# Scores of two heads on different rows of the TensorE array, with keys kept without zero rows

## The chip, the cores and the metric

The kernel runs on one core of a Trainium2 chip. The metric is the time of one execution on the device in microseconds. The core has the engines TensorE (PE, with PEld for its weight loads), VectorE (DVE), ScalarE (ACT), GpSimd (POOL) and the queue SP, which issues transfers.

## What is computed

Two layers of a block on x of 256 x 1024 in f32 come first: a gated feed-forward network, a mixer of three attentions, and a second feed-forward network. Behind them stand a third block (a state-space mixer and short convolutions) and a mixture of experts, which the change leaves alone. The mixer, cut to what matters:

```python
h = rmsnorm(x, mix_norm[l]) @ w_in[l]
o_a = mla_mixer(h_a, ...)    # 6 heads, keys of 64 + 32 columns
o_b = nsa_mixer(h_b, ...)    # 6 heads of 64 columns in 2 key groups of 3 heads
o_c = diff_mixer(h_c, ...)   # 4 heads, each with 2 score products of 32 columns
x = x + jnp.concatenate([o_a, o_b, o_c], axis=-1) @ w_out[l]

# nsa: head (g, r) uses the keys of group g
s_cmp = einsum(q, k_cmp) * scale                 # 15 compressed keys a group
p_cmp = softmax(where(cmp_mask, s_cmp, NEG_BIG)) * cmp_mask
# selection: with 4 blocks of 64 tokens all blocks are taken, so it is causal attention with ks, vs
# window: 512 is longer than the 256 tokens, so it is causal attention with kw, vw
o = g0 * o_cmp + g1 * o_slc + g2 * o_win         # gates from h

# diff
o = softmax(q1 k1) v - lam * softmax(q2 k2) v, then rmsnorm over the head's 64 columns
```

## The kernel before

Everything runs on one core; tokens are two tiles of 128. `_mixer` (line 519) runs once per layer. Its steps stand in a string, `ORDER` (line 40): `w...` are groups of columns of w_in, `mp`, `np` and `dp` prepare the mla, nsa and diff heads, `m0` to `m5`, `n0` to `n5` and `d0` to `d3` are one head each, `df` closes the diff heads. The program's text gives each instruction a place, and a planner in the compiler puts the instructions of each engine into one order by that place and by when their inputs come; so an instruction of a later step can fill a hole of an earlier one. Tiles with a tag share so many buffers, and an instruction that needs a new buffer waits until the old one has been read.

PSUM has eight banks: in the mixer S has 3, T (transposes) 2, O (outputs of a pair of heads) 1, W 2 (line 313). Scores of one head stand in one S bank: queries of token tile 1 against all keys (columns 0 to 255 or 271), queries of tile 0 against the first keys, and masks that are added by a product of an identity with a bf16 mask (`scores`, line 744; `nsa_head`, line 842, for the scores with the 16 compressed columns in front). VectorE then takes maxima (line 725), ScalarE the exponentials with sums (line 729), VectorE and GpSimd scale the rows (line 739), TensorE transposes the probabilities (`ptp`, line 691), VectorE or ScalarE copies them to PT, and the products with the values of two heads write different halves of one O bank (`pv_pair`, line 705; `in_turns`, line 712, keeps such products together behind the first).

An nsa query tile holds two heads, one on rows 0 to 63 and one on rows 64 to 127; a diff query tile holds four score heads of 32 rows. So that a product over all 128 rows gives one head's scores, the keys stand in tiles with zeros on the other rows: `ks` and `kw` (lines 802 to 805), one version per group, filled by half (lines 819, 820), and `kC` (lines 892 to 905), four versions of each of two tiles, filled by quarters by VectorE and ScalarE from the transposed keys `kct` in an S bank. GpSimd writes the zeros.

After the heads, `wo` (lines 972 to 981) multiplies by w_out in four column blocks of two halves; a half stands in a W bank, the other in an S bank. Its eight row chunks are taken in the order `KO`; chunks 3 to 5 are the nsa heads, written in pairs by `store_o`. `fetch` and `cols` issue the transfers on SP into four buffers `st`; `split` makes a high and a low part of each weight on ScalarE and VectorE.

Of the kernel before, what the change touches and what calls it, by code (L numbers as in the profile page):

```python
# [18 lines left out]
T = 256  # L19
# [3 lines left out]
KD = 8  # L23
# [15 lines left out]
LOW.update({k: "vp" for k in ["h3", "g2"]})  # L39
ORDER = "w01 w5 w2 mp m0 m1 w8 w3 w4 w6 np w7 dp m2 m3 d0 d1 n0 n1 d2 d3 n2 n3 n4 n5 m4 df m5"  # L40


class Block:
# [475 lines left out]
    def _mixer(self, l, xops, after):  # L519
# [224 lines left out]
        def scores(s, q, k, kw):  # L744
# [4 lines left out]
            self.mm(s[:, C0], self.identb, self.maskb, False, True)  # L749

        blocks = lambda P: [P[:, i * 128:(i + 1) * 128] for i in range(3)]
        halves = lambda v: [v[:, t * 128:(t + 1) * 128] for t in range(2)]
# [17 lines left out]
        def nsa_prepare():  # L770
# [30 lines left out]

            ks = ap.tile([128, 2, 16 + T], F32, name="ks", tag="hA")
            kw = ap.tile([128, 2, T], F32, name="kw", tag="cqT")
            nc.gpsimd.memset(ks, 0.0)
            nc.gpsimd.memset(kw, 0.0)

# [9 lines left out]
            ACT(qT[:, 2], p2[:, 0:256], scale=0.125)  # L816
            for g in range(2):
                q = slice(g * 64, (g + 1) * 64)
                nc.vector.tensor_copy(ks[q, g, 16:16 + T], p3[q, 0:256])
                nc.vector.tensor_copy(kw[q, g], p3[q, 256:512])  # L820
            p, p2 = self.bank("T", "kcmp"), self.bank("S", "vcmp")
            vcmp = ap.tile([16, 128], F32, name="vcmp", tag="vcmp")
            for g in range(2):
                self.mm(p[g * 64:(g + 1) * 64, 0:15], w2[0:64], h1[0:64, 1, g * 15:(g + 1) * 15])
                self.mm(p2[0:15, g * 64:(g + 1) * 64], h1[64:128, 1, g * 15:(g + 1) * 15], w2[64:128], g == 0, True)
            for g in range(2):
                ACT(ks[g * 64:(g + 1) * 64, g, 0:15], p[g * 64:(g + 1) * 64, 0:15], scale=0.5)
            ACT(vcmp[0:15], p2[0:15, 0:128], scale=0.5)
# [12 lines left out]
                (slice(0, 128), slice(288, 416)), (slice(128, 384), slice(16, 272))]  # L841
        def nsa_head(h):
            qT, ks, kw, vcmp, gt = nsa
            g, hg = divmod(h, 3)
            qt = halves(qT[:, hg])
            im, mb = self.identb, self.maskb

            s = self.bank("S", "S")
            self.mm(s[:, 0:272], qt[1], ks[:, g], True, False)
            self.mm(s[:, 0:16], im, self.cmask[:, 1], False, False)  # L850
            self.mm(s[:, 144:272], im, mb, False, False)
            self.mm(s[:, 272:416], qt[0], ks[:, g, 0:144], False, False)
            self.mm(s[:, 272:288], im, self.cmask[:, 0], False, False)
            self.mm(s[:, 288:416], im, mb, False, True)
            P = ap.tile([128, 416], F32, name="P", tag="P", bufs=6)
            scale_rows(P, SEGC, softmax(s, P, SEGC, gt[:, h, 0:4], -1e29), "c")
            p, pt, n = transposes(blocks(P), "ptp")
            nc.scalar.copy(pt, p[:, 0:n])
            p2 = self.bank("T", "ptc")
            cpt = ap.tile([16, T], F32, name="cpt", tag="cpt", bufs=2)  # L860
            for t in range(2):
                tr(p2[0:16, t * 128:(t + 1) * 128], P[:, 384 + t * 16:400 + t * 16], ident)
            nc.vector.tensor_copy(cpt, p2[0:16, 0:T])
            vc = slice(128 + g * 64, 192 + g * 64)
            pv("s", pt, [hV[:, t, vc] for t in range(2)])
            waiting.setdefault("c", []).append((cpt, vcmp[0:15, g * 64:(g + 1) * 64]))
            if h % 2:
                o = self.bank("O", "opair")
                pv_pair(o, "s", True, False)
                c0, c1 = waiting.pop("c")  # L870
                in_turns([lambda o_=o_, c=c: self.mm(o_, c[1], c[0][0:15], False, False)
                          for o_, c in ((o[64:128, 0:256], c1), (o[0:64, 0:256], c0))])
            s = self.bank("S", "S")
            scores(s, qt, kw[:, g], kw[:, g, 0:128])
            P = ap.tile([128, 384], F32, name="P", tag="P", bufs=6)
            scale_rows(P, SEGS, softmax(s, P, SEGS, gt[:, h, 4:6]), "w")
            p, pt, n = transposes(blocks(P), "ptp")
            nc.vector.tensor_copy(pt, p[:, 0:n])
            vc = slice(256 + g * 64, 320 + g * 64)
            pv("w", pt, [hV[:, t, vc] for t in range(2)])  # L880
            if h % 2:
                pv_pair(o, "w", False, True)
                store_o(3 + h // 2, o[:, 0:256])


        def diff_prepare():
            for t in range(2):
                self.rope(hC[:, t].rearrange("p (h c) -> p h c", h=16)[:, :, 0:8]
                          .rearrange("p h (i f) -> p h i f", i=2), 16, 4, t)
            qC = ap.tile([128, 2, T], F32, name="qC", tag="qC")  # L890

            kC = [ap.tile([128, 4, T], F32, name="kC", tag=tag) for tag in ("kC0", "hC")]
            for k in kC:
                nc.gpsimd.memset(k, 0.0)
            p, p2 = self.bank("T", "qct"), self.bank("S", "kct")
# [12 lines left out]
            return qC, kC, po, pov  # L908

        def diff_head(h):  # L910
            qC, kC, po, pov = dif
            c = h // 2
            Ps = []
            for j in range(2):
                k = kC[c][:, 2 * (h % 2) + j]
                s = self.bank("S", "S")
# [36 lines left out]
        for step in steps:  # L953
# [10 lines left out]
            elif step[0] == "w":  # L964
                w_in_groups([int(c) for c in step[1:]])
                for _ in step[1:]:
                    fetch()
            else:
                {"m": mla_head, "n": nsa_head, "d": diff_head}[step[0]](int(step[1]))
# [947 lines left out]
```

## Time and profile before

| | |
|---|---|
| median of 3 runs | 1529.91 us (1529.60 to 1532.09) |
| the profiled execution | 1532.0 us |
| its span | 1529.8 us |
| TensorE busy | 1492.0 us, 98% of the span |
| VectorE busy | 1025.1 us, 67% |
| ScalarE busy | 729.7 us, 48% |
| GpSimd busy | 91.4 us, 6% |

The profile is of one execution. Busy time is the time in which an engine has an instruction in work, and a busy TensorE is not one at its peak. The chain of waits goes back from the last instruction to what released each step. A view by stretch gives busy time per engine between two moments; an engine that is full in a stretch sets its length, and a share over the whole span can hide that.

### The profile page before, as it was taken

The page shows a single profiled execution, that of the slowest core. Times are in us where ns is not written, and L with a number is a line of the kernel's source. Part 1 is how long each engine was busy: PE and PEld are TensorE (multiplying, and loading weights), DVE is VectorE, ACT ScalarE, POOL GpSimd, SP SyncE. Part 2 cuts the span into 40 slices and gives each one's busy share as a digit, 9 for nine tenths or more (in the row PEclk, how much of TensorE's full clock was granted, in tenths as well). Part 3 has the DMA queues.
Part 4 walks back from the last instruction along what each step waited for, and adds up shares of the span by engine and source line. Part 5 has one row for each costly group of instructions (what it writes and reads, how often), then busy time and mean ns, then how long its engine had stood idle before and what let it go on. Part 6 is the DMA issues. An engine that isn't in the chain of part 4 may idle for free.

```text
span 1529.8 us, 25415 instructions
## 1 busy us (share of the span) xinstructions
PE 1492.0 (98%) x9970; PEld 1253.6 (82%) x9970; DVE 1025.1 (67%) x2013; ACT 729.7 (48%) x1382; POOL 91.4 (6%) x142
## 2 busy tenths in 40 slices
PE   8999999999999999999999999999899999999996
PEld 7999998788999989999888999999799987344432
DVE  6886775868677786778576877779988875122112
ACT  6555565755454555455665655547554442011011
POOL 0000000520000000000025000000510100000000
PEclk9999999999999999999999999999999999999999
DMA  7756664216555565655640555566533588999993
GB/s 252 246 175 193 189 164 145 78 56 205 186 188 193 167 193 192 193 192 164 169 130 2 193 185 176 192 192 207 153 123 116 189 296 336 359 393 393 393 394 117
DMA packets 223559, 308.93 MB, mean 202 GB/s; under 512 B 20908, under 2 KB 167608, under 8 KB 223432
## 3 DMA queue, kind: packets, MB, share of 16 engines
q1 hardware_dynamic: 223128, 306.71, 60.1%
q8 instruction: 80, 1.31, 0.4%
q10 hardware_dynamic: 304, 0.53, 0.1%
q14 instruction: 47, 0.39, 0.1%
HBM read 306.16 MB, written 1.05 MB: 201 GB/s over the span
## 4 chain that ended last, share of the span: by engine, by line
PE 92%; DVE 5%; ACT 1%; issue 1%; DMA 0%; POOL 0%; ACTq 0%; DVEq 0%
PE gu L98 32%; PE acc L98 16%; PE proj L98 6%; PE win L98 6%; PE gate L98 4%; PE y L98 4%; PE up L98 4%; PE h L98 3%; PE wo L98 3%; PE S L98 3%; PE moe L98 1%; PE opair L98 1%; PE ptp L691 1%; PE zp L98 1%; PE xgp L98 1%; DVE wl L167 1%
## 5 line engine op out<-in xcount | busy, mean ns | idle before, releaser
L167 DVE TENSOR_TENSOR wl<-st,wh 128x1024 fp32r<-128x1024 f32 (+1 forms) x370 | 447.5, 1220 | 198.9 <-ACT wh L166 187.7
L166 ACT ACTIVATE wh<-st 128x1024 fp32r<-128x1024 f32 (+1 forms) x382 | 399.3, 1059 | 336.5 <-PE gu L98 134.4
L98 PE MATMUL gu<-xhl,wh 128*128 128x512 f32 (+1 forms) x1440 | 487.8, 392 | 3.1 <-ACT wh L166 2.2
L98 PE MATMUL gu<-xhl,wl 128*128 128x256 f32 x1408 | 381.6, 280 | 0.0
L98 PEld LDWEIGHTS gu<-xhl,wh 128*128 128x128 f32 x1440 | 268.2, 190 | 61.0 <-ACT wh L166 2.6
L98 PEld LDWEIGHTS gu<-xhl,wl 128*128 128x128 f32 x1408 | 260.8, 189 | 0.3
L98 PE MATMUL acc<-hx,wh 128*128 128x256 f32 x1408 | 252.1, 281 | 0.0
L98 PEld LDWEIGHTS acc<-hx,wh 128*128 128x128 f32 x1408 | 216.3, 188 | 1.6
L98 PE MATMUL acc<-hx,wl 128*128 128x256 f32 x704 | 196.8, 281 | 0.0
L98 PE MATMUL proj<-uhl,wh 128*128 128x272 f32 (+2 forms) x592 | 127.6, 306 | 5.3 <-DVE dv L1184 1.6
L98 PEld LDWEIGHTS acc<-hx,wl 128*128 128x128 f32 x704 | 132.6, 188 | 0.0
L98 PE MATMUL win<-wh,xhl 128*128 128x256 f32 (+1 forms) x576 | 109.7, 286 | 0.2 <-DVE xT L410 0.2
L98 PEld LDWEIGHTS proj<-uhl,wh 128*128 128x128 f32 x592 | 95.9, 191 | 10.5 <-ACT cv L1222 2.8
L98 PE MATMUL proj<-uhl,wl 128*128 128x272 f32 (+2 forms) x328 | 95.0, 290 | 0.0
L98 PEld LDWEIGHTS win<-wh,xhl 128*128 128x128 f32 x576 | 90.8, 191 | 4.2 <-issue 3.4
L98 PE MATMUL win<-wl,xhl 128*128 128x256 f32 (+1 forms) x288 | 81.9, 284 | 0.0
L394 ACT ACTIVATE hx<-up 128x512 fp32r<-128x512 f32 x44 | 27.7, 630 | 87.8 <-DVE up L393 87.8
L98 PEld LDWEIGHTS proj<-uhl,wl 128*128 128x128 f32 x328 | 62.5, 191 | 0.2
L1814 DVE SCALAR_TENSOR_TENSOR ys<-y,rc,ys 128x512 fp32r<-128x512 f32 x16 | 11.7, 749 | 67.2 <-ACT ys L1634 66.8
L739 POOL TENSOR_SCALAR P<-P,mx 128x128 f32<-128x128 f32 (+2 forms) x88 | 53.2, 621 | 57.9 <-DVE mx L732 41.8
L729 ACT ACTIVATE P<-S,mx 128x256 f32<-128x256 f32 (+2 forms) x128 | 48.9, 394 | 13.4 <-DVE mx L725 3.6
L98 PEld LDWEIGHTS win<-wl,xhl 128*128 128x128 f32 x288 | 55.0, 191 | 0.3
(522 smaller groups left out, 2133.7 us busy)
## 6 DMA issues: line engine op xcount, KB each, us to landing
st<-ffn_wg SPq DMA_DIRECT2D x44, 1024.0 KB, 5.7
st<-ffn_wu SPq DMA_DIRECT2D x44, 1024.0 KB, 5.4
st<-ffn_wd SPq DMA_DIRECT2D x44, 1024.0 KB, 4.7
st<-w_in SPq DMA_DIRECT2D x36, 1024.0 KB, 5.4
st<-w_out SPq DMA_DIRECT2D x16, 1024.0 KB
mf<-expert_w_gate SPq DMA_DIRECT2D x25, 512.0 KB, 9.8
mf<-expert_w_down SPq DMA_DIRECT2D x21, 512.0 KB, 10.7
mf<-expert_w_up SPq DMA_DIRECT2D x18, 512.0 KB, 11.3
```

What stands on the lines that cost most here:

```text
L98: return self.nc.tensor.matmul(out, lhsT, rhs, start=start, stop=stop, skip_group_check=True)
L166: hi = self.nc.scalar.activation(hl[0], src, AF.Copy)
L167: sub = (self.nc.gpsimd if lo[i] == "p" else self.nc.vector).tensor_sub(hl[1], src, hl[0].bitcast(F32))
L394: nc.scalar.activation(hh, up, AF.Copy)
L691: tr(p[:, i * 128:(i + 1) * 128], b, ident)
L729: nc.scalar.activation(P[:, d], s[:, c], AF.Exp, bias=m[:, 0, i:i + 1], accum_out=m[:, 1, i:i + 1])
L739: (nc.gpsimd if key + str(i) in "c0 c1 c2 d0 d1 m0 w0 w1".split() else nc.vector).tensor_scalar(P[:, d], P[:, d], r[:, i:i + 1], None, op0 ...
L1814: V.scalar_tensor_tensor(yl, py[half], rc[:, 1:2], yh.bitcast(F32), op0=OP.mult, op1=OP.subtract)
```

## The change

Scores of two heads that stand on different rows of the query tile are now issued in turns, each into an S bank of its own: for nsa the heads (0, r) and (1, r) on rows 0 to 63 and 64 to 127, for diff the two score heads of a head, 32 rows each. The product goes over a head's own rows, so the keys need no zeros: `ks`, `kw` and `kC` are single tiles, their memsets go (but for one column of `ks`), and their copies from PSUM are one instruction each. An nsa step is now a pair of heads from both groups; so output chunk 3 + r holds heads r and 3 + r, and w_out's rows are loaded in that order, in four transfers per block in place of one. `ORDER` has three nsa steps in place of six. The diff, cut to its core:

```diff
-ORDER = "w01 w5 w2 mp m0 m1 w8 w3 w4 w6 np w7 dp m2 m3 d0 d1 n0 n1 d2 d3 n2 n3 n4 n5 m4 df m5"
+ORDER = "w01 w5 w2 mp m0 m1 w8 w3 w4 w6 np w7 dp m2 m3 d0 d1 n0 d2 d3 n1 n2 m4 df m5"
...
+        def scores_pair(banks, q, k, rows):
+
+            in_turns([lambda s=s, r=r, c=c, t=t, n=n: self.mm(s[:, c], q[t][r], k[r, 0:n], t == 1, False)
+                      for t, c, n in ((1, C1, 256), (0, C0, 128)) for s, r in zip(banks, rows)])
+            for s in banks:
+                self.mm(s[:, 128:256], self.identb, self.maskb, False, False)
+                self.mm(s[:, C0], self.identb, self.maskb, False, True)
...
-            ks = ap.tile([128, 2, 16 + T], F32, name="ks", tag="hA")
-            kw = ap.tile([128, 2, T], F32, name="kw", tag="cqT")
-            nc.gpsimd.memset(ks, 0.0)
-            nc.gpsimd.memset(kw, 0.0)
+            ks = ap.tile([128, 16 + T], F32, name="ks", tag="hA")
+            kw = ap.tile([128, T], F32, name="kw", tag="cqT")
+            nc.gpsimd.memset(ks[:, 15:16], 0.0)
...
-            for g in range(2):
-                q = slice(g * 64, (g + 1) * 64)
-                nc.vector.tensor_copy(ks[q, g, 16:16 + T], p3[q, 0:256])
-                nc.vector.tensor_copy(kw[q, g], p3[q, 256:512])
+            nc.vector.tensor_copy(ks[:, 16:16 + T], p3[:, 0:256])
+            nc.vector.tensor_copy(kw, p3[:, 256:512])
...
-            for g in range(2):
-                ACT(ks[g * 64:(g + 1) * 64, g, 0:15], p[g * 64:(g + 1) * 64, 0:15], scale=0.5)
+            ACT(ks[:, 0:15], p[:, 0:15], scale=0.5)
...
-        def nsa_head(h):
+        def nsa_pair(hg):
...
+            rows = [slice(64, 128), slice(0, 64)]
+
+            two = [self.bank("S", "S") for _ in range(2)]
+            in_turns([lambda s=s, r=r, t=t, c=c, n=n: self.mm(s[:, c:c + n], qt[t][r], ks[r, 0:n], t == 1, False)
+                      for t, c, n in ((1, 0, 272), (0, 272, 144)) for s, r in zip(two[::-1], rows)])
+            for s in two:
+                self.mm(s[:, 0:16], im, self.cmask[:, 1], False, False)
+                self.mm(s[:, 144:272], im, mb, False, False)
+                self.mm(s[:, 272:288], im, self.cmask[:, 0], False, False)
+                self.mm(s[:, 288:416], im, mb, False, True)
+            for g, s in enumerate(two):
+                h = 3 * g + hg
...
+            two = [self.bank("S", "S") for _ in range(2)]
+            scores_pair(two[::-1], qt, kw, rows)
+            for g, s in enumerate(two):
...
+            pv_pair(o, "w", False, True)
+            store_o(3 + hg, o[:, 0:256])
...
-            kC = [ap.tile([128, 4, T], F32, name="kC", tag=tag) for tag in ("kC0", "hC")]
-            for k in kC:
-                nc.gpsimd.memset(k, 0.0)
+            kC = ap.tile([128, 2, T], F32, name="kC", tag="kC0")
...
-            for c in range(2):
-                for i in range(4):
-                    q = slice(i * 32, (i + 1) * 32)
-                    (nc.vector.tensor_copy if i % 2 else nc.scalar.copy)(kC[c][q, i], p2[q, c * T:(c + 1) * T])
+            nc.vector.tensor_copy(kC, p2[:].rearrange("p (c t) -> p c t", c=2))
...
-            for j in range(2):
-                k = kC[c][:, 2 * (h % 2) + j]
-                s = self.bank("S", "S")
-                scores(s, halves(qC[:, c]), k, k[:, 0:128])
+            two = [self.bank("S", "S") for _ in range(2)]
+            r0 = h % 2 * 64
+            scores_pair(two[::-1], halves(qC[:, c]), kC[:, c], [slice(r0 + 32, r0 + 64), slice(r0, r0 + 32)])
+            for s in two:
...
-        wo = [self.cols(a["w_out"][l], (b * 256, b * 256 + 256)) for b in range(4)]
+
+        def wo_unit(b):
+
+            st = self.wp.tile([128, 2048], F32, name="st", tag="st", bufs=4)
+            v = st[:].rearrange("p (k n) -> p k n", n=256)
+            w = a["w_out"][l][:, b * 256:(b + 1) * 256]
+            rows = lambda r, n, p: w[r:r + n, :].rearrange("(k p) c -> p k c", p=p)
+            nc.sync.dma_start(v[:, 0:3], rows(0, 384, 128))
+            for g in range(2):
+                nc.sync.dma_start(v[g * 64:(g + 1) * 64, 3:6], rows(384 + g * 192, 192, 64))
+            self.loaded = nc.sync.dma_start(v[:, 6:8], rows(768, 256, 128)).ins
+            return st, KD, 256
+
+        wo = [wo_unit(b) for b in range(4)]
```

## Rows read from the trace of the kernel before

**Rows 1.** The page, busy time of engines: us, share of the span, instructions.
```profile
PE 1492.0 (98%) x9970; PEld 1253.6 (82%) x9970; DVE 1025.1 (67%) x2013; ACT 729.7 (48%) x1382; POOL 91.4 (6%) x142
```

**Rows 2.** Windows, layer 0: length, busy PE PEld DVE ACT POOL (count), clock, DMA.
```profile
283.00:300.00 17.00, 17.00 (x138) 13.77 (x137) 15.77 (x73) 13.68 (x64) 10.85 (x17) 1.00 0.01 2
300.00:316.30 16.30, 16.30 (x134) 13.07 (x133) 15.05 (x68) 11.21 (x51) 13.13 (x23) 1.00 0.01 2
316.30:328.60 12.30, 12.30 (x105) 10.33 (x103) 3.91 (x8) 2.41 (x5) 0.00 (x0) 1.00 0.00 1
328.60:342.20 13.60, 13.60 (x115) 13.60 (x114) 10.07 (x18) 9.55 (x14) 0.00 (x0) 1.00 0.34 102
```

**Rows 3.** The same view for layer 1, its second softmax stretch.
```profile
812.70:829.00 16.30, 16.30 (x134) 13.07 (x133) 14.15 (x68) 11.23 (x51) 12.23 (x22) 1.00 0.01 2
```

**Rows 4.** Timeline of TensorE, preparation: start, us, operation, [idle before <-releaser].
```profile
274.90 0.39 PE L98 MATMUL vcmp<-w,h 64*15 64x64 f32 x4 [0.95 <-DVE h L798]
275.23 0.66 PE L900 MATMUL kct<-ident,hC 128*128 128x128 f32 x4
...
278.44 0.70 PE L98 MATMUL S<-kC,qC 128*128 128x256 f32 x2 [0.85 <-ACT P L729]
```

**Rows 5.** Chain that ended last, layer 0: start us, us, what.
```profile
286.25 0.92 PE S L98 x8
...
288.94 1.70 PE S L98 x12
...
297.99 0.80 PE opair L98 x8
298.80 0.48 PE ptp L691 x3
...
306.66 0.34 PE ptp L691 x3
```

**Rows 6.** Timeline of TensorE: the end of one window score set.
```profile
300.60 0.22 PE L98 MATMUL S<-maskb,identb 128*128 128x128 bf16 x1
300.65 0.44 PE L98 MATMUL S<-kw,qT 128*128 128x128 f32 x2
300.93 0.22 PE L98 MATMUL S<-maskb,identb 128*128 128x128 bf16 x1
300.99 0.68 PE L98 MATMUL S<-ks,qT 128*128 128x272 f32 x2
```

**Rows 7.** Instructions on the score tile S: count, ns min/median/max, first and last start.
```profile
L725 DVE TENSOR_REDUCE mx<-S x128: 152/292/422, 250.0 to 824.0; 128x1 f32<-128x128 f32 x52, 128x1 f32<-128x256 f32 x52, 128x1 f32<-128x16 f32 x24
...
L98 PE MATMUL S<-kC,qC x64: 275/354/483, 278.4 to 806.8; 128*128 128x256 f32 x32, 128*128 128x128 f32 x32
```

**Rows 8.** Timeline of VectorE, preparation, columns as in rows 4.
```profile
273.10 0.42 DVE L819 COPY ks<-ktb 64x256 f32<-64x256 f32 x1
...
274.66 0.19 DVE L798 SCALAR_TENSOR_TENSOR h<-h,h 64x30 f32<-64x30 f32 x1
276.31 0.42 DVE L905 COPY kC<-kct 32x256 f32<-32x256 f32 x1 [1.47 <-ACT kC L905]
...
280.67 0.43 DVE L905 COPY kC<-kct 32x256 f32<-32x256 f32 x1
...
281.68 0.55 DVE L762 COPY PT<-ptp 128x384 f32<-128x384 f32 x1
```

**Rows 9.** VectorE's waits, 283 to 316.3 us: total us, times, longest.
```profile
DVE mx L725 <- PE S L98: 1.4, 4, 0.5
```

**Rows 10.** Timeline of the SP queue: DMA issues, start and us.
```profile
238.32 20.70 SPq L150 DMA_DIRECT2D st<-w_out  x4
265.31 0.37 SPq L150 DMA_DIRECT2D st<-ffn_wg  x1
```

**Rows 11.** Instructions on the tile wo: count, ns, first and last start.
```profile
L98 PE MATMUL wo<-ohl,wh x256: 278/283/386, 287.7 to 854.5; 128*128 128x256 f32 x128
```

More of the change, by code (lines that the diff above doesn't have):

```diff
@@ L841, in _mixer @@
                 (slice(0, 128), slice(288, 416)), (slice(128, 384), slice(16, 272))]
-        def nsa_head(h):
+        def nsa_pair(hg):
             qT, ks, kw, vcmp, gt = nsa
-            g, hg = divmod(h, 3)
             qt = halves(qT[:, hg])
             im, mb = self.identb, self.maskb
-            s = self.bank("S", "S")
[L849 to L883, printed above, removed]
@@ new lines, in nsa_pair @@
+            for g, s in enumerate(two):
+                h = 3 * g + hg
+                P = ap.tile([128, 416], F32, name="P", tag="P", bufs=6)
+                scale_rows(P, SEGC, softmax(s, P, SEGC, gt[:, h, 0:4], -1e29), "c")
+                p, pt, n = transposes(blocks(P), "ptp")
+                nc.scalar.copy(pt, p[:, 0:n])
+                p2 = self.bank("T", "ptc")
+                cpt = ap.tile([16, T], F32, name="cpt", tag="cpt", bufs=2)
+                for t in range(2):
+                    tr(p2[0:16, t * 128:(t + 1) * 128], P[:, 384 + t * 16:400 + t * 16], ident)
+                nc.vector.tensor_copy(cpt, p2[0:16, 0:T])
+                pv("s", pt, [hV[:, t, 128 + g * 64:192 + g * 64] for t in range(2)])
+                waiting.setdefault("c", []).append((cpt, vcmp[0:15, g * 64:(g + 1) * 64]))
@@ new lines, in nsa_pair @@
+            o = self.bank("O", "opair")
+            pv_pair(o, "s", True, False)
+            c0, c1 = waiting.pop("c")
+            in_turns([lambda o_=o_, c=c: self.mm(o_, c[1], c[0][0:15], False, False)
+                      for o_, c in ((o[64:128, 0:256], c1), (o[0:64, 0:256], c0))])
+            two = [self.bank("S", "S") for _ in range(2)]
+            scores_pair(two[::-1], qt, kw, rows)
+            for g, s in enumerate(two):
+                P = ap.tile([128, 384], F32, name="P", tag="P", bufs=6)
+                scale_rows(P, SEGS, softmax(s, P, SEGS, gt[:, 3 * g + hg, 4:6]), "w")
+                p, pt, n = transposes(blocks(P), "ptp")
+                nc.vector.tensor_copy(pt, p[:, 0:n])
+                pv("w", pt, [hV[:, t, 256 + g * 64:320 + g * 64] for t in range(2)])
@@ L913, in diff_head @@
             Ps = []
-            for j in range(2):
-                k = kC[c][:, 2 * (h % 2) + j]
-                s = self.bank("S", "S")
-                scores(s, halves(qC[:, c]), k, k[:, 0:128])
+            two = [self.bank("S", "S") for _ in range(2)]
+            r0 = h % 2 * 64
+            scores_pair(two[::-1], halves(qC[:, c]), kC[:, c], [slice(r0 + 32, r0 + 64), slice(r0, r0 + 32)])
+            for s in two:
                 P = ap.tile([128, 384], F32, name="P", tag="P", bufs=6)
@@ L968, in _mixer @@
             else:
-                {"m": mla_head, "n": nsa_head, "d": diff_head}[step[0]](int(step[1]))
+                {"m": mla_head, "n": nsa_pair, "d": diff_head}[step[0]](int(step[1]))
         KO = [int(c) for c in "01345672"]
-        wo = [self.cols(a["w_out"][l], (b * 256, b * 256 + 256)) for b in range(4)]
+        def wo_unit(b):
[9 more added lines that the diff above has]
+        wo = [wo_unit(b) for b in range(4)]
         for b in range(4):
```

## Prediction

> **What bounds the kernel now.** I read from the whole to the stage. The page's engine totals first [rows 1]: TensorE is busy 98% of the span, VectorE 67%. An average over stages with different limits decides nothing, so the next view is the busy time by stretch of the first layer's mixer, the only stage that the change touches (it runs twice, with nearly the same times). There the reader is to see three regimes [rows 2]. From 283.0 to 316.3 us, where the softmaxes are, TensorE has no idle time, but VectorE is busy 15.77 of 17.00 and 15.05 of 16.30 us: two engines are full at once, and only 1.23 + 1.25 = 2.5 us of VectorE's time is free (in layer 1's second stretch 14.15 of 16.30 are busy [rows 3]). From 316.3 to 342.2 VectorE has room and TensorE none: here the products with w_out that were left over run, and TensorE alone sets the end. Before 283.0, in the preparation of the nsa and diff heads, neither is full; TensorE stands twice in a row of waits, 0.95 us for VectorE's h and 0.85 us for a score bank that ScalarE reads [rows 4].
>
> So a cheaper score on TensorE is worth what VectorE can follow in the softmax stretch, plus what goes from the preparation, and not simply the TensorE time that is saved. The w_out products fill TensorE's holes, but until the last score has been read only those of the first column block can (the other column block wants an S bank), so holes in the softmax stretch mostly stay holes.
>
> **Scores, part by part.** A plain set of scores (256 + 128 columns and two masks) is 1.70/2 = 0.85 us in the chain, a set with the compressed keys 0.92 us [rows 5]. Within a set the masks are short: from the start of one to the next product 0.05 to 0.06 us [rows 6]. Per layer the change pairs 3 window pairs, 4 diff pairs (64 records for kC over two layers, two records a product, two products a set: 8 sets a layer [rows 7]) and 3 pairs with compressed keys.
>
> The trace of before has no two products on different rows at once. The nearest row is the pair on different columns: opair, 256 + 128 columns for two heads, 0.80 us [rows 5], where the same two heads one after the other would need 2 x (0.85 - 0.11) = 1.48 us by a score set without its masks. I take 0.80 for two heads on different rows. What follows such a pair starts late: three transposes right behind opair take 0.48 us, elsewhere 0.34 [rows 5], so 0.14 us is charged per pair. Plain pair after: 0.80 + 4 masks x 0.055 + 0.14 = 1.16 us against 1.70, saved 0.54. Compressed pair: 0.80 x 416/384 = 0.87, 8 masks x 0.055 = 0.44, 0.14: 1.45 against 1.84, saved 0.39. A layer: 7 x 0.54 + 3 x 0.39 = 5.0 us of TensorE. Bounds: without overlap the plain pair is 1.48 + 0.22 + 0.14 = 1.84, a loss of 0.14 each or 1.4 us a layer; without the late start the saving is 6.4.
>
> The Trainium skill (TensorE: Matmul & The Clock Gate, Part 3, measured speedup) lists four row tiles at 3.07 times one; read as 77% of the ideal, an estimate from that page would make the products of a plain pair 1.48/1.54 = 0.96 instead of 0.80 us and the layer's saving 3.3 us; no row here shows products on different rows. Both prices are above what VectorE can follow, so my sum is the same by either.
>
> **Preparation.** VectorE copies ks and kw in four copies of 64 rows, 0.42 us each and overlapping, from 273.10 to 274.66, so 0.39 apart, ahead of the h that TensorE waits 0.95 us for [rows 4, 8]; two copies of all 128 rows do it after, at the same price each (copies of 32 and of 64 rows both take 0.42 [rows 8], so the rows are free as far as is shown). h comes 2 x 0.39 = 0.78 us earlier, and I count 0.75. kC goes from four copies on VectorE and four on ScalarE to one on VectorE of 128x512; a 128x384 copy is 0.55 us, and 128 columns more by the slope from the 256-column copies 0.68 [rows 8]. VectorE saves 4 x 0.42 - 0.68 = 1.0 us. More than that, the bank with the transposed keys is read until 280.67 + 0.43 = 281.1 us by the last copy [rows 8]; after, it is free one copy behind the transposes that end at 275.23 + 0.66 [rows 4], near 276.6, and it is one of the three S banks in which scores stand. The first diff score waits 0.85 us for a bank; with a bank free and no key copies between the exponentials on ScalarE, I take 0.75 of that. Preparation: -1.5 us a layer. From both sides: the w_in products could fill the first hole already (0), or the whole 1.8 us and the 1.0 us of VectorE go (-2.8).
>
> **Softmax stretch.** VectorE's work there is unchanged: same reductions, scalings and copies. It can only lose idle time, 2.5 us in layer 0, and 2.15 in the second stretch of layer 1 alone [rows 2, 3]. Waits that are named as "reductions wait for scores" are 1.4 us [rows 9]; the rest are short gaps between dependent steps. I take the 1.4 and 0.4 of the rest: -1.8 us a layer. TensorE then has more than 5.0 - 1.8 us of holes or filler in it, which pay nothing.
>
> **Costs put at nothing.** The removed memsets stand on GpSimd, which waits there; nothing on the path waits for them now. w_out comes in 4 transfers per block instead of 1: 16 issues at 0.37 us a layer instead of 4, 4.4 us more of the SP queue. The four are issued between 238.3 and 259.0 us, the next issue on that queue is at 265.3 [rows 10] and the first product with w_out at 287.7 [rows 11]; each block is a few us later at worst, and the next layer's weights queue behind it with 6 us of room. If that cover went, the price is about 1.1 us for the last block. The order of heads and of w_out's rows moves no work by itself: chunk 3 is still the first pair of nsa heads. The output bank is held by the pair from selection to window products, as before.
>
> **Sum.** -1.5 - 1.8 = -3.3 us a layer, -6.6 us in all. The profiled execution took 1532.0 us, of which 1529.8 is the span: 1525.4 by its own time. The median of the runs is 1529.9, 2.1 lower; against it 1523.3 us.
>
> **Rivals.**
>
> 1. *Everything counts.* TensorE's saving is passed on in full, since VectorE's order also changes and fillers move into the holes: 5.0 + 1.8 of idle time = 6.8 us a layer, 1516.3 us. For it: VectorE has free time after 316.3. Against it: VectorE's 93% in the stretch [rows 2] and the two engines' dependence on each other. Chance 0.12.
>
> 2. *Two banks at once* (the other side). A pair starts when two of three S banks are free, so that while TensorE writes a pair (1.16 us) only one head waits in a bank, and its reductions keep VectorE for 2 x 0.29 us [rows 7]. Before, a single head started with one free bank and two heads were ahead. What VectorE has not covered with scalings and PT copies is up to 1.16 - 0.58 = 0.58 us a pair, 5.8 us a layer. With the preparation's -1.5 that is up to +4.3 a layer: 1538.5 us. It decides from about 0.4 us of VectorE idle per pair (2.5 us are there now, 1.5 come back in the preparation, over 10 pairs). Half of it, 0.2 to 0.4, eats the gain and leaves no measurable difference. Chance of slower 0.13, of no difference by this 0.18. For it: the three banks, and the reductions that already wait for scores [rows 9]. Against it: VectorE is 93% busy, with plenty of other heads' work in its queue, and the kct bank comes back earlier. The Trainium skill (TensorEngine Tiling (Array Packing), Restrictions and Gotchas) says that row tiles raise the pressure on PSUM, as different row tiles must write different banks; this change gives each head of a pair its own bank for that, and no row here shows yet what it costs.
>
> 3. *The rows don't overlap.* The change doesn't do what it says: +1.4 - 1.5 us a layer, with VectorE's idle time left as it is, 1529.7 us. For it: no row shows overlap of rows. Against: columns overlap nearly in full [rows 5]. Chance 0.05.
>
> **How the numbers follow.** Likeliest is the sum, 1523.3 us, chance 0.52 (1520 to 1526.8). About 0.2% (3 us) is what a measurement of this kernel can tell from no change: faster is the forecast and rival 1, 0.64; within 0.2% is half of rival 2 and rival 3, 0.23; slower 0.13. The range reaches from rival 1 to where rival 2 begins to lose, 1516 to 1532: 13 in 100 lie above it, a few below.
>
> **What the profile after would show.** In the timeline two S products with the same start to within some ns, and about 1.2 us per plain pair: right, and if the second starts where the first ends, rival 3. TensorE with idle time between 283 and 313 us, VectorE above 95% busy there: the forecast. TensorE full and the stretch some 5 us shorter: rival 1. VectorE's reductions waiting for S in gaps of 0.4 us and more, S products waiting for ScalarE's exponentials: rival 2. h and the first diff score each about 0.75 us earlier against the last w_in product: the preparation's step. The stretch of w_out products after the last opair stays at 13.6 us [rows 2]; if it doesn't, the fillers were mis-sized. What would make the prediction wrong above all is the order of instructions on TensorE, which the program's planner makes anew: if it puts many w_out products elsewhere or the transposes of one head behind the next pair, the gaps move by more than my terms.

## The result and the profile after

The change makes the kernel slower: 1547.85 us in the median of 11 runs (1535.51 to 1575.19), against 1530.02 us before (1529.56 to 1533.05); the ratio is 1.0067 [1.0042, 1.0093], from which the four longest runs (1563 us and more) are left out; the median of the other seven is 1538.23 us. The spread is the first thing to see. Five runs lie between 1535.5 and 1538.4 us, at a mean granted clock of 0.994 to 0.997; the run of 1547.9 us had 0.987, that of 1550.9 us 0.985, the four longest 0.966 to 0.977. So there are two questions: what costs some 8 us with the clock at its upper level, and what takes the clock away.

The profiled execution (1537.75 us, span 1536.0) is one of the first kind. From the first product with w_in to the end of the last with w_out a mixer takes 144.56 and 144.07 us, against 140.65 and 140.15 before: +3.9 us in each of the two layers, with the granted clock at 1.00 throughout. All of the loss is there; the rest of the execution is 1.7 us shorter than in the profile before. The page, busy time of engines, against [rows 1]:

```profile
PE 1498.6 (98%) x9970; PEld 1253.0 (82%) x9970; DVE 1021.7 (67%) x2003; ACT 725.0 (47%) x1372; POOL 86.1 (6%) x136
```

TensorE is busy for 6.6 us more, where the scores were to cost 10 us less. The windows of layer 0 that answer to [rows 2] (the same columns: length, then busy time and count of PE, PEld, DVE, ACT, POOL, the granted clock, DMA):

```profile
281.20:298.00 16.80, 16.30 (x118) 12.06 (x114) 13.26 (x58) 11.11 (x52) 10.33 (x17) 1.00 0.00 1
298.00:316.80 18.80, 18.42 (x133) 13.23 (x132) 16.24 (x78) 11.97 (x58) 7.44 (x15) 1.00 0.01 2
316.80:331.50 14.70, 14.29 (x122) 12.28 (x120) 5.26 (x15) 3.43 (x11) 5.27 (x9) 1.00 0.00 1
331.50:345.10 13.60, 13.60 (x115) 13.60 (x114) 10.04 (x18) 9.55 (x14) 0.00 (x0) 1.00 0.33 102
```

VectorE was to become the bound; it fell to 79% and 86% of the two softmax stretches (93% and 92% before), and TensorE is still nearly full. VectorE now waits for TensorE: its reductions wait 2.2 us for scores where [rows 9] had 1.4. The row is of VectorE's waits from 281.0 to 316.8 us (total, times, longest):

```profile
DVE mx L725 <- PE S L98: 2.2, 5, 0.8
```

TensorE's timeline of the preparation and the first diff scores shows why (start us, us, operation):

```profile
273.06 0.39 PE L98 MATMUL vcmp<-w,h 64*15 64x64 f32 x4
273.38 0.66 PE L902 MATMUL kct<-ident,hC 128*128 128x128 f32 x4
...
275.67 0.92 PE L98 MATMUL S<-kC,qC 32*128 32x256 f32 x4
276.52 0.28 PE L98 MATMUL S<-maskb,identb 128*128 128x128 bf16 x2
276.73 0.92 PE L98 MATMUL S<-kC,qC 32*128 32x256 f32 x4
277.58 0.29 PE L98 MATMUL S<-maskb,identb 128*128 128x128 bf16 x2
277.80 0.92 PE L98 MATMUL S<-kC,qC 32*128 32x256 f32 x4
```

No two heads are in turns. Four records of one head (two f32 products) are followed by that head's masks, and only then comes the next head; all 20 sets of a layer stand so. The bank of the lead, the head whose product stands first in the program's text, comes free first, so its own products can go while the partner's bank is still being read, and the planner lets them. ScalarE's timeline shows the reading that holds the other two banks when the first diff score starts at 275.67:

```profile
275.97 0.46 ACT L729 ACTIVATE P<-S,mx 128x256 f32<-128x256 f32 x1
...
276.85 0.47 ACT L729 ACTIVATE P<-S,mx 128x256 f32<-128x256 f32 x1
```

These are the last readings of the two mla heads ahead, until 276.4 and 277.3 us. Counted so, sets written against sets read, two of the three banks were still in use at the start of the lead in nine of the ten pairs of each layer; in the tenth the partner's bank had come free 0.2 us before.

A lone plain set takes 276.73 to 277.80, 1.07 us; before it was 0.85 [rows 5]. One set each of before and after, with the operation behind it:

```profile
279.99 0.60 PE L98 MATMUL S<-kC,qC 128*128 128x256 f32 x2
...
280.82 0.50 PE L691 MATMUL ptp<-ident,P 128*128 128x128 f32 x3
```

```profile
284.30 0.92 PE L98 MATMUL S<-kw,qT 64*128 64x256 f32 x4
...
285.28 0.83 PE L98 MATMUL po<-hW,PT 128*128 128x64 f32 x6
```

Looking into the records, there is extra time going in and coming out: from the last full-height f32 product to the first on 32 or 64 rows 0.20 us pass instead of 0.11, and from the last of these to the mask 0.20 where the 128 columns need 0.11. The set's own step, from its first record to the next operation, is 0.97 instead of 0.82, and the 0.15 more with the 0.09 ahead of it are 0.24 us a set. TensorE pays for going from products on all rows to products on some rows and back. 20 sets x 0.24 = 4.8 us a layer.

The preparation did what was forecast. VectorE, against [rows 8]:

```profile
272.02 0.42 DVE L824 COPY ks<-ktb 128x256 f32<-128x256 f32 x1
272.37 0.41 DVE L825 COPY kw<-ktb 128x256 f32<-128x256 f32 x1
272.81 0.19 DVE L806 SCALAR_TENSOR_TENSOR h<-h,h 64x30 f32<-64x30 f32 x1
274.07 0.69 DVE L904 COPY kC<-kct 128x512 f32<-128x512 f32 x1 [1.07 <-PE kct L902]
```

Both of TensorE's waits of [rows 4] are gone, and the first diff score stands 1.8 us earlier against the start of the mixer (75.07 us behind it, 76.85 before).

### The profile page after: what moved, and what is told of

Its sections match the earlier page's. It is cut to its first block, busy times and chain, and to the rows that moved or that the text cites. A ratio compares the mean times of both kernels' runs of the same rounds, so it can differ in the third digit from the quotient of the medians.

```text
span 1536.0 us, 25422 instructions
## 1 busy us (share of the span) xinstructions
PE 1498.6 (98%) x9970; PEld 1253.0 (82%) x9970; DVE 1021.7 (67%) x2003; ACT 725.0 (47%) x1372; POOL 86.1 (6%) x136
## 4 chain that ended last, share of the span: by engine, by line
PE 92%; DVE 5%; ACT 2%; issue 1%; DMA 0%; ACTq 0%; DVEq 0%
PE gu L98 32%; PE acc L98 16%; PE proj L98 7%; PE win L98 6%; PE gate L98 4%; PE y L98 4%; PE up L98 4%; PE S L98 3%; PE h L98 3%; PE wo L98 3%; PE moe L98 1%; PE opair L98 1%; PE zp L98 1%; PE xgp L98 1%; PE ptp L691 1%; DVE wl L167 1%
## 5 line engine op out<-in xcount | busy, mean ns | idle before, releaser
L739 POOL TENSOR_SCALAR P<-P,mx 128x128 f32<-128x128 f32 (+1 forms) x88 | 53.6, 633 | 120.8 <-DVE mx L732 88.8
L729 ACT ACTIVATE P<-S,mx 128x128 f32<-128x128 f32 (+2 forms) x128 | 48.9, 399 | 22.6 <-DVE mx L725 12.0
```

The source lines that it names most:

```text
L729: nc.scalar.activation(P[:, d], s[:, c], AF.Exp, bias=m[:, 0, i:i + 1], accum_out=m[:, 1, i:i + 1])
L739: (nc.gpsimd if key + str(i) in "c0 c1 c2 d0 d1 m0 w0 w1".split() else nc.vector).tensor_scalar(P[:, d], P[:, d], r[:, i:i + 1], None, op0 ...
```

## Experiments

### The same kernel once more

> The changed kernel once more, for the comparison with the runs beside it. In its trace no two score products of a pair start together: 20 sets a layer each go alone over their own rows, 1.07 us for a plain set from product to product where the kernel before needs 0.86. Theory A (switching): each lone set pays a change from products over all rows to products over some rows and back, about 0.2 us plain and 0.3 us with compressed keys, 14 x 0.2 + 6 x 0.3 = 4.6 us a layer, 9.2 us in all, of which the quicker preparation gives 2.8 back: +6 us against the kernel before. Theory B (order): the steps in pairs and the new order of heads cost the 6 us, rows cost nothing. Both expect the same time here, 1.003 to 1.006 of the kernel before.

1556.03 us in the median of 4 runs (1538.18 to 1565.80; the kernel before beside it 1530.51), ratio 1.0108 [1.0041, 1.0175]. The sample lies above the 1.003 to 1.006 expected; its shortest run, 1.005 of the kernel before, lies in it. The profiled execution took 1556.35 us, and its windows show the second part of the loss:

```profile
275.00:279.00 4.00, 4.00 (x25) 3.04 (x24) 2.79 (x11) 1.80 (x8) 1.37 (x2) 1.00 1.09 365
279.00:300.00 21.00, 21.00 (x87) 15.82 (x85) 10.02 (x44) 9.33 (x44) 6.06 (x11) 0.50 0.03 11
300.00:320.00 20.00, 20.00 (x80) 12.84 (x78) 8.57 (x35) 5.25 (x21) 5.49 (x8) 0.50 0.00 1
320.00:334.00 14.00, 13.63 (x99) 9.80 (x98) 12.13 (x60) 10.51 (x53) 7.06 (x13) 1.00 0.01 2
```

For 41.0 us, from 279.0 to 320.0, the granted clock is 0.50, the lower of its two levels (1.2 instead of 2.4 GHz), right through the softmax stretch; this mixer takes 161.8 us, the next, at the full clock, 144.1. Against 144.6 us for the same mixer in the first profile, a microsecond at the lower level cost 17.3/41.0 = 0.42 us. Measured from the start of the mixer, every instruction of TensorE up to 279.3 us starts within 0.05 us of its place in the first profile of the same kernel, where the clock stayed at 1.00. The instructions do not decide whether it falls in one execution. The profile of the kernel before has no such stretch in its mixers.

### Back to zero rows, all else changed

```diff
-            ks = ap.tile([128, 16 + T], F32, name="ks", tag="hA")
+            ks = ap.tile([128, 2, 16 + T], F32, name="ks", tag="hA")
...
-            scores_pair(two[::-1], qt, kw, rows)
+            for g, s in enumerate(two):
+                scores(s, qt, kw[:, g], kw[:, g, 0:128])
```

> Everything of the change but the rows: keys with zero rows again and products over all 128 rows, head after head; pairs as steps, order of heads, w_out in four transfers and chunk order as changed. Theory A: a plain set is 0.85 us again, the 9.2 us go, the preparation's 2.8 us go too: the time of before within 2 us, 1528 to 1532. Theory B: still 5 to 8 us above the kernel before, 1535 to 1538.

1529.99 us (1529.52 to 1532.08, 10 runs), ratio 0.9999 [0.9990, 1.0009]. The order of the heads, the steps by pairs, the other chunk order and the four transfers per block of w_out cost nothing that the interval of 0.1% would show. Both parts of the loss need the scores on a head's own rows.

### Masks first, so that pairs must meet

```diff
+            for s in banks[::-1]:
+                self.mm(s[:, 128:256], self.identb, self.maskb, True, False)
+                self.mm(s[:, C0], self.identb, self.maskb, False, False)
-            in_turns([lambda s=s, r=r, c=c, t=t, n=n: self.mm(s[:, c], q[t][r], k[r, 0:n], t == 1, False)
+            in_turns([lambda s=s, r=r, c=c, t=t, n=n: self.mm(s[:, c], q[t][r], k[r, 0:n], False, t == 0)
                       for t, c, n in ((1, C1, 256), (0, C0, 128)) for s, r in zip(banks, rows)])
-            for s in banks:
-                self.mm(s[:, 128:256], self.identb, self.maskb, False, False)
-                self.mm(s[:, C0], self.identb, self.maskb, False, True)
```

With the masks ahead of all products (for the nsa pairs in the same way), both banks are taken before the first product.

> The masks go first into the two banks of a pair and the products follow, so that the first product cannot be issued before both banks are there; now the four products of a pair stand next to each other on TensorE. Theory A: two products on different rows overlap, a plain pair takes 0.80 + 0.22 + 0.3 = about 1.3 us instead of 2 x 1.07, TensorE gains 0.8 us a pair, 8 us a layer against the changed kernel; VectorE can follow with 3 to 5 of it: 1522 to 1532. Theory C (two banks at once): waiting for two of three banks leaves VectorE idle by 0.4 us and more per pair: 1536 and above, though the products overlap. Theory D (rows never overlap): a pair takes 1.44 + 0.22 + 0.3 = 2.0 us: 1534 to 1538.

1550.13 us (1546.92 to 1555.85), ratio 1.0132 [1.0104, 1.0160]. Now the two heads do run side by side. TensorE's timeline of masks_first, one diff pair:

```profile
815.84 0.27 PE L98 MATMUL S<-maskb,identb 128*128 128x128 bf16 x2 [0.62 <-ACT P L729]
816.05 0.92 PE L98 MATMUL S<-kC,qC 32*128 32x256 f32 x8
816.90 0.55 PE L691 MATMUL ptp<-ident,P 128*128 128x128 f32 x3
```

The eight records of two heads take the time that four took in the changed kernel; the starts of two heads are 0.007 us apart. But the pair had to wait 0.62 us for its second bank, and the granted clock was 0.50 for 13.6 us in each layer.

### The same with full-height products and zero rows

The edit against masks_first, without the keys' copies, which are those of the kernel before:

```diff
-            in_turns([lambda s=s, r=r, c=c, t=t, n=n: self.mm(s[:, c], q[t][r], k[r, 0:n], False, t == 0)
+            in_turns([lambda s=s, k=k, c=c, t=t, n=n: self.mm(s[:, c], q[t], k[:, 0:n], False, t == 0)
```

> Masks first, two heads' products in turns as in masks_first, each pair waiting for two free banks, but with zero-row keys and full-height products, so nothing can run side by side and nothing switches rows. Theory 3 (waiting for two banks is what lost the time of masks_first, by idle TensorE): the gaps of TensorE in the softmax part stay, as large as there (some 4 us of a 25 us stretch), the array time of a pair goes back to 1.7 us, so some 1540 to 1545 us with the clock at 1.0 throughout. If idle time alone brings the halved clock, halved stretches appear here too and the time is over 1548. Theory 4 (the halved clock needs products on part of the rows): no halved stretch beyond those of the kernel before.

1551.34 us (1549.11 to 1554.83), ratio 1.0133 [1.0114, 1.0151]. The mixers take 151.3 and 150.6 us, 10.5 more than before, with the clock at 0.50 for 3.4 us a layer only. TensorE's timeline of pairs_full_rows:

```profile
296.44 0.27 PE L98 MATMUL S<-maskb,identb 128*128 128x128 bf16 x2 [0.53 <-ACT P L729]
296.55 1.52 PE L98 MATMUL S<-kC,qC 128*128 128x256 f32 x8
297.91 0.49 PE L691 MATMUL ptp<-ident,P 128*128 128x128 f32 x3
```

With transposes behind both, a pair takes 1.47 us from the first of these masks to the next operation here and 1.06 us in masks_first: running two heads on different rows saves 0.41 us a pair, going in and coming out included. The windows tell what that is worth, first of masks_first, then of pairs_full_rows:

```profile
276.00:300.00 24.00, 19.53 (x142) 13.43 (x142) 16.50 (x65) 12.61 (x59) 11.60 (x18) 0.86 0.13 43
300.00:325.00 25.00, 21.01 (x159) 16.19 (x158) 19.92 (x88) 13.98 (x67) 11.16 (x21) 0.86 0.00 1
```

```profile
276.00:300.00 24.00, 18.72 (x130) 15.15 (x129) 16.93 (x65) 13.65 (x63) 10.10 (x17) 0.93 0.17 55
300.00:325.00 25.00, 21.74 (x167) 16.78 (x166) 20.53 (x91) 14.54 (x70) 12.54 (x23) 1.00 0.00 1
```

In both kernels TensorE is idle for some 8.5 of 49 us, and VectorE for 11.5 to 12.6. The waits of TensorE between 276 and 325 us name the most of it, for masks_first and for pairs_full_rows (total, times, longest):

```profile
PE S L98 <- ACT P L729: 5.1, 6, 2.6
```

```profile
PE S L98 <- ACT P L729: 5.1, 7, 1.2
```

Scores wait for a bank that ScalarE still reads, with full-height products just as with products on own rows. The 1540 to 1545 us expected of theory 3 were too few: waiting for two of three banks makes the layer 10.5 us longer, with 1.4 of them for the clock (3.4 x 0.42, an estimate). By these waits, that waiting for two banks costs time stands; the rest of the idle time stands behind engines that work on the same scores. Full height and idle time do not bring the long halved stretches.

### Four score banks

The kernel masks_first with another share of the PSUM banks:

```diff
-        with self.phase(f"mixer{l}", **dict(S=3, T=2, O=1, W=2)):
+        with self.phase(f"mixer{l}", **dict(S=4, T=2, O=1, W=1)):
```

> As with the masks first, with four score banks in place of three and one W bank in place of two. If waiting for two banks at once is what costs (theory C), it is 2 us a layer faster than with three banks; if not, it is the same or slower by the w_out products that can no longer fill holes before the diff heads are closed, 1 us a layer.

1549.94 us (1549.56 to 1551.61), ratio 1.0127 [1.0110, 1.0144]. The mixers take 149.6 and 150.9 us. TensorE's idle time between 270 and 347 us shrinks from 9.3 us in masks_first to 6.2, but the first w_out product comes 116.4 us behind the start of the mixer instead of 83.1, since the only W bank is taken, and the clock is 0.50 for 10.2 us a layer. By its own expectation (2 us a layer faster, if two banks at once are what costs) the run speaks against that theory; but it took away filler too, more than the 1 us expected, so it decides nothing. That the missing filler takes what the bank gives is the likely reading, not a shown one.

### Own rows for a part of the heads

In nsa_rows the diff heads, in diff_rows the nsa heads go back to zero rows, as in zero_rows:

```diff
-            scores_pair(two[::-1], halves(qC[:, c]), kC[:, c], [slice(r0 + 32, r0 + 64), slice(r0, r0 + 32)])
+            for j, s in enumerate(two):
+                k = kC[c][:, 2 * (h % 2) + j]
+                scores(s, halves(qC[:, c]), k, k[:, 0:128])
```

> Of the changed kernel, only the 12 score sets a layer with 64-row keys (selected, compressed and window heads) run on their own rows; the 8 difference sets go back to keys with zero rows. Theory 1 (each switch of TensorE between products on some rows and products on all rows costs time): at the full clock a lone set costs some 0.24 us more than before (0.15 in its own step, 0.09 in the gap ahead of it, both from the changed kernel's trace), so 12 x 0.24 = 2.9 us a layer, less some 0.5 of the preparation that stays (the difference keys' copies are back): +2.4 a layer, 1535 us where the granted clock stays at 1.0. Theory 2 (the halved clock comes with the 32-row products of the difference heads, which stood right before its fall): no halved stretch in the softmax part, all runs within 2 us of 1535. Rival to 2 (any products on part of the rows bring it): some runs longer than 1537, up to 1555, with halved stretches in the softmax part.

> The other half: only the 8 difference sets a layer run on their own 32 rows; the 12 sets with 64-row keys have zero rows and full-height products. Theory 1: 8 x 0.24 = 1.9 us a layer, less some 0.9 of the preparation (8 key copies become 1): +1.0 a layer, 1532.5 us where the granted clock stays at 1.0. Theory 2: halved stretches behind the difference sets, runs of 1535 to 1550. Rival to 2: all runs within 2 us of 1532.5.

nsa_rows: 1538.65 us (1536.31 to 1540.68, 4 runs), ratio 1.0053 [1.0036, 1.0070]; diff_rows: 1536.13 us (1532.23 to 1540.58, 10 runs), ratio 1.0027 [1.0015, 1.0040]. At the full clock the mixer grows by 4.6 us with the 12 nsa sets and by 1.4 us (layer 1) with the 8 diff sets; expected were 2.4 and 1.0. The price per set is as expected in either (0.97 instead of 0.82 in a plain set's own step, 0.20 instead of 0.11 ahead of it), so theory 1 stands. nsa_rows exceeds it by holes: as expected, the wait ahead of the first diff score is back there (0.91 us), but three holes of 0.65, 0.38 and 0.29 us follow in the softmax stretch, where the changed kernel has 0.25 and 0.13, and 0.35 and 0.41 behind it. These five are 2.1 us, which with the 2.4 makes 4.5. The two parts don't add up to the whole (+3.9), since each has holes of its own (0.6 us in diff_rows, 1.1 in the changed kernel).

The clock stayed at 1.00 in both mixers of the profile of nsa_rows (1536.31 us); two of its other runs took 1540.5 and 1540.7 us at a mean clock of 0.994 instead of 0.997, above what theory 2 allows, and no trace shows where. In the profile of diff_rows it was 0.50 from 273.7 us on:

```profile
273.70:290.80 17.10, 17.10 (x66) 12.02 (x67) 7.19 (x24) 6.40 (x27) 2.87 (x4) 0.50 0.35 117
290.80:305.00 14.20, 13.98 (x106) 11.00 (x105) 11.86 (x58) 9.05 (x43) 9.95 (x16) 1.00 0.01 2
```

TensorE's timeline there:

```profile
273.66 0.58 PE L98 MATMUL vcmp<-w,h 64*15 64x64 f32 x4 [0.93 <-DVE h L806]
...
278.52 1.65 PE L98 MATMUL S<-kC,qC 32*128 32x256 f32 x4
```

The fall came behind the hole of the preparation, almost 5 us ahead of the first score on 32 rows, so these cannot have started it. zero_rows, with full-height scores, falls at the same place in layer 1 (73.2 us behind the start of the mixer; 73.4 in diff_rows), but is back after 3.4 us:

```profile
786.90:790.30 3.40, 3.40 (x14) 2.61 (x14) 1.11 (x4) 1.00 (x4) 0.95 (x1) 0.50 1.07 364
790.30:804.00 13.70, 13.02 (x99) 10.52 (x98) 12.77 (x54) 11.15 (x52) 5.74 (x10) 1.00 0.13 42
```

### 64 rows in place of 32

```diff
-            scores_pair(two[::-1], halves(qC[:, c]), kC[:, c], [slice(r0 + 32, r0 + 64), slice(r0, r0 + 32)])
+            r = slice(r0, r0 + 64)
+            scores_pair(two[::-1], halves(qC[:, c]), [kC[c][:, 1], kC[c][:, 0]], [r, r])
```

> Like diff_rows (only the 8 difference sets a layer on part of the rows), but on 64 rows, of which a key fills 32 and the other 32 are zero; the key copies of the kernel before are back. Switches as in diff_rows. Theory 2 (the halved clock comes with 32-row products): no halved stretch in the softmax part, all runs within 2 us of 1534 (1532.3 of the best diff_rows runs and some 1.8 us of two layers' preparation back), against 1532 to 1541 in diff_rows. Rival (any part of the rows, or the place and order of these sets): runs spread over 8 us as in diff_rows, with halved stretches of 3 to 17 us.

> The changed kernel whole, but the difference heads' products on 64 rows (half of them zero in the key) instead of 32. Theory 2: no halved stretch, all runs within 2 us of 1538 (the changed kernel at the full clock 1536 and some 1.8 of preparation back), where the changed kernel spread from 1535.5 to 1575. Rival: a spread like the changed kernel's, runs over 1545.

diff_64_rows: 1541.62 us (1537.12 to 1545.39), ratio 1.0074 [1.0045, 1.0102], with the clock at 0.50 from 273.9 us for 17.1 us. all_64_rows: 1561.02 us (one run at 1539.37, three at 1561), ratio 1.0148 [1.0074, 1.0222], with 0.50 for 44.4 us in layer 1, from 76.8 us behind the mixer's start. Theory 2 falls: the halved clock is no matter of 32-row products. all_64_rows has 64-row products alone and the longest stretch so far.

### Twice as many switches

```diff
-            in_turns([lambda s=s, r=r, c=c, t=t, n=n: self.mm(s[:, c], q[t][r], k[r, 0:n], t == 1, False)
-                      for t, c, n in ((1, C1, 256), (0, C0, 128)) for s, r in zip(banks, rows)])
-            for s in banks:
+            for s, r in zip(banks, rows):
+                self.mm(s[:, C1], q[1][r], k[r, 0:256], True, False)
                 self.mm(s[:, 128:256], self.identb, self.maskb, False, False)
+                self.mm(s[:, C0], q[0][r], k[r, 0:128], False, False)
                 self.mm(s[:, C0], self.identb, self.maskb, False, True)
```

> The changed kernel with each head's mask product put back between its two score products, so that every one of the 20 sets a layer goes from products on all rows to products on its own rows and back twice instead of once. Theory 1 (the switch has a price, 0.24 us a set in and out): another 20 x 0.24 = 4.8 us a layer, so the mixer stage of the profile goes from 143.9 to some 148.7 us where the granted clock is 1.0, and the best runs from 1536 to some 1545.5 us. Rival (the 3.9 us a layer come from other things, as the softmax engines waiting for heads in another order): the same work in the same order, so 144 us a layer and 1536 in the best runs.

1597.04 us (1589.64 to 1604.78), ratio 1.0436 [1.0390, 1.0482]. Where its clock was 1.00, TensorE's timeline gives the price:

```profile
334.86 0.70 PE L98 MATMUL S<-kw,qT 64*128 64x256 f32 x2
335.49 0.23 PE L98 MATMUL S<-maskb,identb 128*128 128x128 bf16 x1
335.65 0.49 PE L98 MATMUL S<-kw,qT 64*128 64x128 f32 x2
336.07 0.23 PE L98 MATMUL S<-maskb,identb 128*128 128x128 bf16 x1
336.14 0.39 PE L691 MATMUL ptp<-ident,P 128*128 128x128 f32 x2
```

The set takes 334.86 to 336.14, 1.27 us by the records. With one switch it was 0.97, with none 0.82. A second switch costs 0.30 us where 0.24 was expected: theory 1 stands, and the rival is out, since the work is the same. But the best run lies 44 us above the 1545.5 expected for it, and the windows show the clock there:

```profile
280.10:324.50 44.40, 44.40 (x157) 25.83 (x158) 17.82 (x77) 13.99 (x65) 11.50 (x18) 0.50 0.00 1
819.40:867.20 47.80, 47.80 (x172) 28.54 (x171) 19.36 (x82) 15.92 (x73) 11.50 (x18) 0.50 0.01 4
870.60:887.70 17.10, 17.10 (x63) 9.89 (x64) 9.71 (x49) 7.57 (x36) 5.53 (x10) 0.50 0.00 1
```

109 us at the lower level in this profile, in both layers, and mean clocks of 0.951 to 0.963 in all four runs. At 0.42 us for each, 109 us are worth some 46 us, an estimate; this execution lies 49 us above the expected time. TensorE's records leave no idle time in it, so no hole that the profile shows holds the clock down.

### The zeros in the queries

```diff
-            self.mm(s[:, 0:272], qt[1], ks[:, g], True, False)
+            self.mm(s[:, 0:272], qt[1], ks, True, False)
...
-            ACT(qT[:, 0:2], p[:].rearrange("p (h t) -> p h t", h=2), scale=0.125)
+                ACT((q0, q1)[g][q, 0:2], p[q].rearrange("p (h t) -> p h t", h=2), scale=0.125)
```

The kernel before with full-height products head after head, but the zero rows stand in the queries: keys are copied in one piece each, the query copies go by heads.

> The kernel before with the zero rows moved from the keys into the queries: full-height products, head after head, but the keys are copied once as they come, and the preparation copies the queries by heads instead. Theory 5 (the preparation's gain, 1.4 us a layer in the changed kernel's trace, is real and does not need products on part of the rows; it comes from fewer key copies ahead of the first scores): up to 2.8 us less in two layers, 1527.7. Rival: the query copies take the place of the key copies on the same engines ahead of the same first scores, so 1530 to 1531, no change.

1528.10 us (1526.48 to 1529.61, 10 runs), against 1531.45 of the kernel before beside it; ratio 0.9981 [0.9972, 0.9991]. The preparation's gain is real and needs no products on own rows. TensorE's timeline:

```profile
273.27 0.39 PE L98 MATMUL vcmp<-w,h 64*15 64x64 f32 x4
...
275.79 0.65 PE L98 MATMUL S<-kC,qC 128*128 128x256 f32 x2
...
277.15 0.70 PE L98 MATMUL S<-kC,qC 128*128 128x256 f32 x2 [0.32 <-ACT P L729]
```

The hole ahead of vcmp is gone and of the 0.85 us ahead of a diff score 0.32 are left. The first diff score is 1.9 us earlier, the end of the mixer 1.0 us: half is lost again, probably in the softmax stretch, where TensorE is full and VectorE nearly so:

```profile
292.00:309.00 17.00, 17.00 (x139) 13.70 (x137) 16.20 (x77) 13.49 (x63) 12.70 (x23) 1.00 0.01 3
```

This is the one version here that beats both kernels.

## Why the prediction was wrong, point by point

**The pair of scores (failed).** The step "I take 0.80 for two heads on different rows" priced a pair that exists in the array, but not in this kernel. masks_first shows that the price was good: four masks at 0.055, 0.09 going in and 0.85 for the products make 1.16 us, as forecast. What failed is that two heads would start together: the lead needs one bank, gets it first, and goes alone, so TensorE lost 4.8 us a layer where it was to gain 5.0. The prediction named the planner's order as what would make it wrong above all, yet gave that no chance and no price.

**The bound without overlap (failed).** It was +0.14 us a pair, from one late start behind opair [rows 5]. Measured is 0.24 a set, so 0.48 a pair: each lone set is entered and left by itself, and entering costs too. So rival 3, at +1.4 us a layer from the scores, had the right course, one head after the other, at a third of its price: 4.8. The Trainium skill (TensorEngine Tiling (Array Packing), Tiling Modes) says that a change of tiling mode drains TensorE. The trace agrees, with 0.20 us instead of 0.11 both going in and coming out. The late transposes behind opair, 0.48 instead of 0.34 [rows 5], look like the same price on columns, and the prediction charged it once a pair.

**Preparation (right).** -1.5 us a layer was forecast, and the first diff score came 1.8 us earlier, with both waits gone. Without the other changes, and with the queries copied by heads in the keys' place (query_zeros), it brings 1.0 us a layer at the end.

**Softmax stretch (failed).** -1.8 us a layer hung on a cheaper TensorE, with VectorE above 95% busy. The bound stayed TensorE, which got dearer, and VectorE fell to 79% and 86%.

The ledger of a layer at the full clock: 20 x 0.24 = +4.8 for the switches, -1.8 for the preparation, and +1.1 for four new holes (0.25, 0.13, 0.35, 0.41 us): +4.1, measured +3.9. The two layers make 7.8 us, which puts the kernel at 1537.8 from the median before. The median of the seven runs behind the ratio is 1538.2; the median of all eleven lies another 10 us above the ledger.

**The clock (missing).** Those 10 us were in no term and no rival. What the runs show: stretches at the lower level that are longer than 3.4 us stood in a mixer only with scores on own rows (zero_rows has one of 3.4 us and query_zeros none, and every run of theirs lies between 1526.5 and 1532.1 us). With lone sets the clock falls in or behind the preparation, 73 to 80 us into a mixer (once more at 129 us with twice the switches), and then stays down for 17 to 48 us, or does not fall at all; with pairs that meet it falls for 3.4 to 10.2 us at a time, 83 to 117 us into it. With twice the switches it is down for 109 us of one execution. pairs_full_rows, with 8.5 of 49 us idle, has 3.4 us a layer. That the switches hold it down fits all this, and the number of switches was varied; but why it falls in one execution of the same instructions and not in the next, and whether the switches or the rows left unused weigh more, stays open. diff_64_rows and all_64_rows exclude only that it takes 32-row products.

**Rival 2, two banks at once.** In the changed kernel it did not happen, because pairs did not meet. Where they were made to meet it did: masks_first lies 9.9 us a layer above the kernel before, of which 13.6 x 0.42 = 5.7 us are the clock, an estimate; the other 4.2 are close to the rival's +4.3. pairs_full_rows, without the overlap and without the quicker preparation, lies 10.5 above. So none of the ways tried was good: alone, the sets pay the switch; together, they pay the bank.

**Put at nothing (right, as far as is shown).** Transfers and order: zero_rows is at 0.9999 of before. The memsets are back in it, so no run tests them alone; the ledger leaves nothing for them. One size was off: the twelve further issues of w_out took 0.6 to 0.8 us each and not 0.37, so 7.8 us a layer of the SP queue in place of 4.4, and the cover held, with the last one done at 260.3 us and the next issue at 264.3. The last stretch of w_out products is 13.6 us as before.

## What to carry to other kernels

Before two products are to share TensorE's array, look up in the planned order what the second waits for: if it waits for a buffer of its own, it comes late, and the first goes alone. Charge every set on part of the rows for entering and leaving (0.24 us here); a pair that did meet still saved 0.41 us with that price paid once. And a zero row can be moved to the operand whose copies are off the path: that alone, without any new way of multiplying, gave 0.2%.

## What was not expected of the hardware

Going from f32 products on all 128 rows to products on 32 or 64 rows and back costs 0.24 us, and a second change within the same set 0.30. Two heads on different rows start 0.007 us apart and take the time of one (0.85 us from the first record to the next operation, against 1.36 one after the other at full height). TensorE's granted clock can stay at the lower of its two levels for 41 to 48 us while the engine's records show no idle time (44.40 of 44.40 us busy), and the same instructions at the same times are met at either level from one execution to the next.
